# Loading four operands through GpSimd's queue into the tiles that they are split in

## The chip, the cores and the metric

The kernel runs on one core of one Trainium2 chip. The metric is the device time of one execution in microseconds (us); lower is better.

## What is computed

One layer of an encoder trunk on 1,024 tokens of width 1,024, with 16 learned meta tokens put in front. In outline:

```
a = rms_norm(h)
[q,k,v | q,f_fwd,f_bwd,i,g | gate_na, gate_hg] = a @ W_in
A  = W_na_out( neighbourhood attention(q, k, v) )
Bm = W_hg_out( bidirectional HGRN2 recurrence(q, f_fwd, f_bwd, i, g) )
h  = h + W_o( sigmoid(gate_na) * A + sigmoid(gate_hg) * Bm )
h  = h + W_down( relu(rms_norm(h) @ W_up)^2 )
out = rms_norm(h), meta tokens dropped
```

The change lies in the two gates, `sigmoid(a @ W_gate)` for 2,048 columns.

## The kernel before

Every float32 product is made as three products of float32r operands: an operand is split into a high part (a rounded copy, made by ScalarE) and a low part (the operand minus its high part, made by VectorE). The helper is `split(hi, lo, src)`, lines 95 to 97: line 96 is ScalarE's copy, line 97 VectorE's subtraction. Both parts must be there before TensorE can use the operand.

The stages follow one another: norm and transposition of `a` into the tiles `aT` (two halves of 512 tokens, each with a high and a low tile of 128 x 8 x 512), the recurrence (to about 350 us), attention in four pairs of heads (to about 597 us), the gates, the two output projections, the MLP. The gates use Winograd's seven products for 2 x 2 blocks. The activations' blocks are `b11` and `b21` (the first half of the tokens as it stands in `aT`), `b22` (the lower half of the second) and four sums of blocks, `t1` to `t4`, the second operands. The sums are made piece by piece during attention by `block_sums`: GpSimd adds high and low parts back together, subtracts, and stores each of the 4 x 4 pieces (128 x 512 float32, 256 KB) in DRAM as `tsp[v][k]`.

In the gates stage the first two products of each of eight column pairs need `b11` and `b21` alone; they are `first_gates`, each with its own weight block (`load_block`: SP loads `raw`, line 125 is ScalarE's copy `hi`, line 126 VectorE's subtraction `lo`). Eight blocks pass through two pairs of `hi` and `lo` buffers, so a block's parts are made just when the block before the last has been used up. Then `gate_pair` runs eight times with the other five products, in the order b22, t2, t1, t3, t4 (the last one delayed behind the next pair's first). Before these stands `second_operand(v)`, for t2, t1, t3 and t4 in this order: for each of its four pieces SP loads `tsp[v][k]` into a staging tile `gv`, of which there are five, and `split` makes the high and low pieces from it. `t2`'s parts go into the upper halves of the second `aT` tiles (the projections of attention and `block_sums` have to be done with them); `t1`, `t3` and `t4` have tiles of their own, called `at` in the trace, in the pool `gpr`. The five `gv` tiles are used again in `gate_pair` for its results `u1`, `u3`, `u2`.

The pool `gpr` takes the place of attention's pool `npr`; both end where the pool `gfp` begins. By the sizes in the code `npr` has 46,912 bytes a partition (`Vn` 9,216, then `OT` 4,096, five `pr` of 1,728, small tiles, `PT0` and `PT1` of 11,264 each, `low` 2,048) and `gpr` 53,248 (six `at` tiles of 8,192, two `p3` of 2,048), so `gpr` starts 6,336 bytes below `npr`. `t1`'s low tile then covers bytes 1,856 to 10,048 of `npr`, the end of `Vn` and the beginning of `OT`; `t3`'s high tile covers `OT` and `pr`, its low tile `pr` and `PT0`; `t4`'s tiles cover `PT0` and `PT1`. A tile is written for the first time when the tiles that lay there are done with; `OT` is done with when its store to DRAM (`osp`, line 673, on GpSimd's queue) has landed.

The order of the instructions on each engine is not that of the code up to the last product of the MLP: a planner orders them by its own estimate of durations, takes the earliest in the code among those that it takes to be ready, and lets later ones go ahead into gaps. On the chip each engine, and each engine's DMA queue, then works strictly in that order.

Of the kernel before, what the change touches and what calls it, by code (L numbers as in the profile page):

```python
# [9 lines left out]
F32 = mybir.dt.float32  # L10
F32R = mybir.dt.float32r
# [7 lines left out]
P = 128  # L19
# [3 lines left out]
TH = 512  # L23
# [25 lines left out]
def layer(ctx: ExitStack, tc: tile.TileContext, x, meta, w_in, w_na, w_hg, w_o, w_up, w_dn,  # L49
          g_mix, g_mlp, g_fin, gain, bias, lbl, lmask, wmask, out):  # L50
    nc = tc.nc
    pe, act, dve, pool, sp = nc.tensor, nc.scalar, nc.vector, nc.gpsimd, nc.sync
# [42 lines left out]
    def split(hi, lo, src):  # L95
        act.copy(hi, src)  # L96
        dve.tensor_tensor(lo, src, hi.bitcast(F32), op=ALU.subtract)  # L97
# [128 lines left out]
    tsp = {v: [dramp.tile([P, TH], F32, name=f"tsp_{v}_{k}") for k in range(4)] for v in ("t1", "t2", "t3", "t4")}  # L226
# [301 lines left out]
    with (tc.tile_pool(name="npr", bufs=1, side="right", reuse_waits="tile") as npr,  # L528
# [18 lines left out]
        for p in range(NPAIR):  # L547
            NB = npl.tile([P, 2, 1024], F32, tag="NB", name="NB")
            for i in range(2):
# [3 lines left out]
                for o, j0, m in ((0, 0, 3), (432, 1, 2), (720, 0, 2)):  # L553
                    a = NB[:, i, o:o + m * SW].rearrange("p (j c) -> p j c", c=SW)[:, :, :P]
# [140 lines left out]
    def up_bank(t):  # L695
# [4 lines left out]
    aV = {"b11": [t[:, :4, :TH] for t in aT[0]], "b21": [t[:, 4:, :TH] for t in aT[0]],  # L700
          "t2": [t[:, :4] for t in aT[1]], "b22": [t[:, 4:] for t in aT[1]]}
# [5 lines left out]
    def flat(t):  # L707
        return t.rearrange("p k c -> p (k c)")
# [25 lines left out]
    gpr = gps.enter_context(tc.tile_pool(name="gpr", bufs=1, side="right", reuse_waits="tile"))  # L734

    def g_tile(tag, n, dt=F32, bufs=1):
        return gp.tile([P, n], dt, tag=tag, name=tag, bufs=bufs)

    def second_operand(v):
        for k in range(4):  # L740
            t = g_tile("gv", TH, bufs=5)
            if v not in aV:
                aV[v] = [gpr.tile([P, 4, TH], F32R, name=f"a{v}{q}") for q in range(2)]
            sp.dma_start(t, tsp[v][k])
            split(aV[v][0][:, k], aV[v][1][:, k], t)

    w_turn = [0]

# [54 lines left out]
    for v in ("t2", "t1", "t3", "t4"):  # L803
        second_operand(v)
# [25 lines left out]
    for br, wsrc in enumerate((w_hg, w_na)):  # L830
        for jj in range(0, KC, 2):
            raw, hi, lo = (flat(wp.tile([P, KC, P], dt, tag=t, name=t))
                           for t, dt in (("raw", F32), ("hi", F32R), ("lo", F32R)))
# [5 lines left out]
            for j in (jj, jj + 1):  # L839
                sg = sgp.tile([P, T], F32, tag="sg", name="sg")  # L840
                sp.dma_start(sg, gsp[8 * br + j])
                for h in range(2):
                    pm = mm_tile()
                    t = slice(h * TH, (h + 1) * TH)
# [119 lines left out]
    def a_tile(pool_, tag, dt=F32, bufs=1, n=TH):  # L964
        return pool_.tile([P, n], dt, tag=tag, name=tag, bufs=bufs)
# [89 lines left out]
    for m in range(NP):  # L1055
# [3 lines left out]
        for v in ("s1", "s3"):  # L1059
            t = a_tile(upw, "sx", bufs=2, n=D).rearrange("p (k c) -> p k c", c=P)  # L1060
# [215 lines left out]
    with tc.manual_schedule(engines={sp.engine, dve.engine, act.engine, pool.engine}):  # L1276
# [5 lines left out]
        for n, (p_, m) in enumerate(steps):  # L1282
# [13 lines left out]
            elif m < NP // 2 - 2:  # L1296
                a, b = cur
# [72 lines left out]
```

## Time and profile before

| what | value |
|---|---|
| median of 3 runs | 1552.63 us (1550.44 to 1553.09) |
| profiled execution: its time | 1550.2 us |
| profiled execution: span from first to last instruction | 1548.4 us |
| TensorE (PE) busy | 1502.1 us, 97% of the span |
| VectorE (DVE) busy | 1008.4 us, 65% |
| ScalarE (ACT) busy | 654.7 us, 42% |
| GpSimd (POOL) busy | 401.8 us, 26% |
| mean granted clock of TensorE | 0.998 of 2.4 GHz |

The profiled execution took 1.8 us more than its span and 2.4 us less than the median. In the rows, a time is counted from the start of the span; "idle before" is how long the engine had nothing to do ahead of an instruction, and behind the arrow stands what ended it. SPq, POOLq and ACTq are the DMA queues of SyncE, GpSimd and ScalarE.

### The profile page before, as it was taken

How to read it: one execution, taken by the hardware profiler on the slowest of the kernel's cores; microseconds unless marked ns; L12 is line 12 of the kernel's file. 1: busy time of each engine (PE TensorE's matmuls, PEld its weight loads, DVE VectorE, ACT ScalarE, POOL GpSimd, SP SyncE). 2: the span in 40 equal slices, each digit the busy share in tenths (PEclk: the TensorE clock that was granted, in tenths of full speed). 3: DMA queues.
4: the chain of work that ended last, by engine and by line, in shares of the span. 5: the costliest groups of instructions: out<-in, count | busy, mean ns of one | idle time of the engine just before them, and what ended most of it. 6: DMA issues, size and time to landing. Idle time of an engine off the chain costs nothing.

```text
span 1548.4 us, 23448 instructions
## 1 busy us (share of the span) xinstructions
PE 1502.1 (97%) x9188; PEld 1253.5 (81%) x9188; DVE 1008.4 (65%) x1592; ACT 654.7 (42%) x1168; POOL 401.8 (26%) x359
## 2 busy tenths in 40 slices
PE   6999999999999998999999999999999999999998
PEld 5788888878888887888888887888888788887886
DVE  6666666664876877666475369666666444879566
ACT  6231313124665666334122245555555433434444
POOL 4413131315315310011000032444444200237033
PEclk9999999999999999999999999999999999999999
DMA  5101010113123128434951324444444576563224
GB/s 181 43 28 56 28 56 28 55 29 128 49 72 119 55 69 272 136 123 163 339 178 41 109 91 148 165 155 153 153 150 148 169 273 233 190 231 107 98 82 150
DMA packets 142335, 195.61 MB, mean 126 GB/s; under 512 B 8064, under 2 KB 90112, under 8 KB 142224
## 3 DMA queue, kind: packets, MB, share of 16 engines
q1 hardware_dynamic: 133856, 173.40, 33.8%
q10 hardware_dynamic: 6192, 13.37, 2.2%
q0 software_dynamic: 2176, 7.34, 1.3%
q8 instruction: 72, 1.18, 0.3%
q14 instruction: 39, 0.32, 0.1%
HBM read 139.55 MB, written 54.53 MB: 125 GB/s over the span
## 4 chain that ended last, share of the span: by engine, by line
PE 83%; DVE 9%; issue 3%; ACT 2%; DMA 2%; POOL 1%; DVEq 0%; POOLq 0%; SPq 0%; ACTq 0%
PE mm L135 11%; PE mm L136 10%; PE mm L137 10%; PE mm L1112 4%; PE pa L1112 4%; PE pb L691 4%; PE pb L692 4%; PE pb L693 4%; PE pc L1112 4%; PE pb L1112 4%; PE pc L693 2%; PE pc L692 2%; PE pc L691 2%; PE pa L692 2%; PE pa L691 2%
## 5 line engine op out<-in xcount | busy, mean ns | idle before, releaser
L135 PE MATMUL mm<-aT,hi 128*128 128x512 f32 (+2 forms) x640 | 230.2, 360 | 2.7 <-DVE QX L563 1.5
L137 PE MATMUL mm<-aT,lo 128*128 128x512 f32 (+2 forms) x640 | 227.8, 356 | 0.0
L136 PE MATMUL mm<-aT,hi 128*128 128x512 f32 (+2 forms) x640 | 226.6, 354 | 0.0
L97 DVE TENSOR_TENSOR dl<-ur,dh 128x1024 fp32r<-128x1024 f32 x55 | 76.6, 1393 | 93.7 <-ACT dh L96 93.5
L135 PEld LDWEIGHTS mm<-aT,hi 128*128 128x128 f32 x640 | 121.9, 191 | 17.2 <-issue 1.7
L137 PEld LDWEIGHTS mm<-aT,lo 128*128 128x128 f32 x640 | 121.8, 190 | 13.5 <-POOL lo L126 0.3
L136 PEld LDWEIGHTS mm<-aT,hi 128*128 128x128 f32 x640 | 121.9, 190 | 12.4
L96 ACT CAST dh<-ur 128x1024 fp32r<-128x1024 f32 x55 | 57.9, 1053 | 162.5 <-issue 78.1
L125 ACT CAST hi<-raw 128x1024 fp32r<-128x1024 f32 x36 | 37.8, 1051 | 106.7 <-PE mm L136 75.6
L974 ACT CAST wh<-sx 128x512 fp32r<-128x512 f32 x70 | 42.5, 618 | 94.7 <-DMA sx<-in_w_up 33.1
L975 DVE TENSOR_TENSOR wl<-sx,wh 128x512 fp32r<-128x512 f32 x70 | 51.2, 738 | 31.0 <-ACT wh L974 31.0
L975 DVE TENSOR_TENSOR wl<-raw,wh 128x512 fp32r<-128x512 f32 x46 | 50.2, 1090 | 23.7 <-ACT wh L974 22.9
L979 ACT ACTIVATE uv<-uv 128x512 f32<-128x512 f32 x48 | 30.4, 632 | 67.4 <-DVE uv L1090 50.0
L1095 POOL TENSOR_TENSOR us<-u,uv 128x512 f32<-128x512 f32 x15 | 24.0, 1603 | 133.4 <-ACT uv L980 133.4
L1202 POOL TENSOR_TENSOR w<-w,tt 128x512 f32<-128x512 f32 x16 | 23.3, 1458 | 134.0 <-DVE tt L1201 120.4
L399 POOL TENSOR_TENSOR Y<-X,TN 128x512 f32<-128x512 f32 x20 | 35.0, 1749 | 86.1 <-DVE X L396 86.1
L691 PE MATMUL pb<-nt,wh 128*128 128x512 f32 x128 | 50.4, 394 | 3.6 <-DVE uv L1083 2.6
L126 DVE TENSOR_TENSOR lo<-raw,hi 128x1024 fp32r<-128x1024 f32 x34 | 43.2, 1270 | 15.6 <-ACT hi L125 15.4
L92 POOL TENSOR_SCALAR rtm<-ssq 128x1 f32<-128x1 f32 (+1 forms) x17 | 6.4, 376 | 180.4 <-ACT junk L924 156.0
L618 DVE CUSTOM_DVE_ANT_0 pr<-nsc,NB 128x432 f32<-128x432 f32 (+1 forms) x64 | 35.2, 559 | 26.6 <-PE nsc L613 26.5
L1112 PE MATMUL mm<-dl,dh 128*128 128x512 f32 x126 | 49.9, 396 | 2.1 <-DVE dl L97 2.1
L135 PE MATMUL mm<-o,hi 128*128 128x512 f32 x128 | 50.0, 390 | 0.6 <-DVE mix L850 0.6
(380 smaller groups left out, 4409.3 us busy)
## 6 DMA issues: line engine op xcount, KB each, us to landing
raw<-in_w_in SPq DMA_DIRECT2D x56, 512.0 KB, 3.9
ur<-usp SPq DMA_DIRECT2D x55, 512.0 KB, 3.5
raw<-in_w_up SPq DMA_DIRECT2D x16, 1024.0 KB, 5.5
usp<-us SPq DMA_DIRECT2D x60, 256.0 KB, 2.0
sg<-gsp SPq DMA_DIRECT2D x16, 512.0 KB, 4.3
w<-in_w_dn SPq DMA_DIRECT2D x16, 512.0 KB, 4.5
usp<-uv SPq DMA_DIRECT2D x30, 256.0 KB, 2.2
gsp<-gv ACTq DMA_DIRECT2D x24, 256.0 KB, 2.4
```

Source lines behind the costliest of these rows:

```text
L96: act.copy(hi, src)
L97: dve.tensor_tensor(lo, src, hi.bitcast(F32), op=ALU.subtract)
L126: eng.tensor_tensor(lo[:, :kc], raw[:, :kc], hi[:, :kc].bitcast(F32), op=ALU.subtract)
L135: pe.matmul(ps, lh, rh, start=first, stop=False)
L136: pe.matmul(ps, lh, rl, start=False, stop=False)
L137: pe.matmul(ps, ll, rh, start=False, stop=last)
L691: pe.matmul(ps, lhs[0][:, c], rhs[0][:, k], start=first and k == 0, stop=False, skip_group_check=True)
L692: pe.matmul(ps, lhs[0][:, c], rhs[1][:, k], start=False, stop=False, skip_group_check=True)
L693: pe.matmul(ps, lhs[1][:, c], rhs[0][:, k], start=False, stop=k == 3, skip_group_check=True)
L974: act.copy(v(hi), src)
L975: dve.tensor_tensor(v(lo), src, v(hi).bitcast(F32), op=ALU.subtract)
L1112: pe.matmul(ps, a[n == 2][:, q, j * P:(j + 1) * P], b[n == 1][:, q], start=first and n == 0, stop=last and n == 2, skip_group_check=True)
```

## The change

`second_operand` has no staging tile any more. The tiles of `t1`, `t3` and `t4` are made at the start. Each piece is loaded by GpSimd's queue instead of SP's, straight into the place of its low part; `split` then copies the high part from there, and the subtraction overwrites the loaded piece with the low part. The five `gv` tiles stay for `gate_pair`.

```
     def second_operand(v):
+        if v not in aV:
+            aV[v] = [gpr.tile([P, 4, TH], F32R, name=f"a{v}{q}") for q in range(2)]
         for k in range(4):
-            t = g_tile("gv", TH, bufs=5)
-            if v not in aV:
-                aV[v] = [gpr.tile([P, 4, TH], F32R, name=f"a{v}{q}") for q in range(2)]
-            sp.dma_start(t, tsp[v][k])
-            split(aV[v][0][:, k], aV[v][1][:, k], t)
+            hi, lo = (t[:, k] for t in aV[v])
+            pool.dma_start(lo.bitcast(F32), tsp[v][k])
+            split(hi, lo, lo.bitcast(F32))
```

## Rows read from the trace of the kernel before

**Rows 1.** The page: busy time of the engines, and the chain that ended last by engine.

```profile
PE 1502.1 (97%) x9188; PEld 1253.5 (81%) x9188; DVE 1008.4 (65%) x1592; ACT 654.7 (42%) x1168; POOL 401.8 (26%) x359
...
PE 83%; DVE 9%; issue 3%; ACT 2%; DMA 2%; POOL 1%; DVEq 0%; POOLq 0%; SPq 0%; ACTq 0%
```

**Rows 2.** Busy time by stretches of the span: end of attention, its tail, `first_gates`, the first gate pair, the other pairs. Columns: stretch, its length, then busy us of PE, PEld, DVE, ACT and POOL with counts, granted clock, DMA share, GB/s.

```profile
555.00:575.00 20.00, 19.96 (x122) 16.86 (x122) 19.02 (x58) 15.30 (x39) 0.00 (x0) 1.00 0.12 34
575.00:590.00 15.00, 12.57 (x71) 10.01 (x70) 12.26 (x32) 12.91 (x24) 0.00 (x0) 1.00 0.65 218
590.00:613.00 23.00, 21.10 (x96) 16.93 (x94) 16.69 (x26) 15.23 (x27) 0.54 (x1) 1.00 0.84 270
613.00:640.00 27.00, 26.91 (x119) 22.30 (x120) 16.39 (x23) 10.78 (x17) 1.60 (x1) 1.00 0.51 151
640.00:740.00 100.00, 99.62 (x439) 81.99 (x438) 63.79 (x82) 42.06 (x56) 12.01 (x7) 1.00 0.46 148
```

**Rows 3.** What TensorE waited for from 555 to 640 us (total us, times, longest).

```profile
PE ppt L633 <- DVE PT L645: 2.4, 1, 2.4
PE mm L691 <- ACT hi L125: 1.5, 1, 1.5
PE mm L693 <- DVE lo L126: 0.5, 1, 0.5
```

**Rows 4.** The chain of waits in order of time, the load and what follows it on ScalarE (start, us, what).

```profile
602.40 6.04 DMA gv<-tsp_t
...
610.25 0.59 ACT go L712
```

**Rows 5.** ScalarE's instructions in order of time (start, us).

```profile
600.74 0.61 ACT L96 CAST at<-gv 128x512 fp32r<-128x512 f32 x1
601.25 0.62 ACT L96 CAST at<-gv 128x512 fp32r<-128x512 f32 x1
...
602.73 1.66 ACT L96 CAST at<-gv 128x512 fp32r<-128x512 f32 x3
604.96 0.59 ACT L724 COPY g<-mm 128x512 f32<-128x512 f32 x1 [0.57 <-PE mm L693]
608.46 1.88 ACT L96 CAST at<-gv 128x512 fp32r<-128x512 f32 x3 [2.91 <-DMA gv<-tsp_t]
...
610.74 1.04 ACT L125 CAST hi<-raw 128x1024 fp32r<-128x1024 f32 x1
```

**Rows 6.** VectorE's instructions in order of time, in attention's tail.

```profile
585.72 0.69 DVE L660 COPY low<-pov 64x512 f32<-64x512 f32 x1 [1.57 <-PE pov L658]
586.34 0.68 DVE L682 TENSOR_TENSOR sx<-raw 128x512 f32<-128x512 f32 x1
587.05 0.68 DVE L662 TENSOR_TENSOR OT<-pov,low 64x512 f32<-64x512 f32 x1
587.65 1.27 DVE L645 TENSOR_TENSOR PT<-ppt,PT 128x512 fp32r<-128x512 f32 x2
```

**Rows 7.** The instructions on the tiles `gv` (duration in ns min/median/max, first and last start in us).

```profile
L744 SPq DMA_DIRECT2D gv<-tsp_t x16: 319/354/1073, 581.5 to 610.5; - x16
L96 ACT CAST at<-gv x12: 610/622/631, 600.7 to 616.7; 128x512 fp32r<-128x512 f32 x12
L97 DVE TENSOR_TENSOR at<-gv,at x12: 684/689/694, 601.7 to 617.4; 128x512 fp32r<-128x512 f32 x12
...
L786 DVE TENSOR_TENSOR gv<-gv,pc x8: 678/680/689, 633.8 to 727.6; 128x512 f32<-128x512 f32 x8
```

**Rows 8.** What SP's queue waited for from 560 to 640 us (total us, times, longest).

```profile
SPq L744 <- DVE aT L97: 3.5, 4, 2.0
...
SPq L744 <- DVE at L97: 2.7, 4, 1.3
```

**Rows 9.** TensorE's first matmuls with t2 (`aT`, into `pb`), t1, and t4 (`at`) in the first gate pair.

```profile
626.37 0.39 PE L691 MATMUL pb<-aT,hi 128*128 128x512 f32 x1
...
629.09 0.39 PE L691 MATMUL pc<-at,hi 128*128 128x512 f32 x1
...
637.25 0.39 PE L691 MATMUL pb<-at,hi 128*128 128x512 f32 x1
```

**Rows 10.** GpSimd's instructions in order of time.

```profile
597.07 0.54 POOL L673 DMA_DIRECT2D osp<-OT  x1 [50.74 <-DVE OT L662]
636.50 1.60 POOL L790 TENSOR_TENSOR gv<-gv,p 128x512 f32<-128x512 f32 x1 [38.90 <-DVE gv L789]
```

**Rows 11.** DMA issues of the whole span (KB each, median us from issue to landing).

```profile
tsp_t<-rt POOLq DMA_DIRECT2D x16, 256.0 KB, 2.4
gv<-tsp_t SPq DMA_DIRECT2D x16, 256.0 KB, 5.1
```

**Rows 12.** The DMA engines from 594 to 613 us: what they moved, and two kinds of issue in it.

```profile
DMA packets 5223, 5.67 MB, mean 299 GB/s; under 512 B 273, under 2 KB 3355, under 8 KB 5222
...
raw<-in_w_in SPq DMA_DIRECT2D x2, 512.0 KB, 6.6
osp<-OT POOLq DMA_DIRECT2D x1, 512.0 KB, 4.4
```

**Rows 13.** The chain of waits in order of time: the last projection of attention that the chain holds, and the last products of attention's values.

```profile
552.36 0.23 PE mm L136
...
593.79 0.23 PE pov L658
```

## The prediction

> **What bounds the kernel now.** I read the page first: TensorE is busy for 97% of the span and holds 83% of the chain that ended last [rows 1]. A change that leaves TensorE's work alone can only win what TensorE idles, so the second view is the busy time by stretches around the gates [rows 2]. From 613 us on TensorE is full: 26.91 of 27 us, then 99.62 of 100. What can be won lies before, in the 38 us from 575 to 613, where it is busy for 12.57 + 21.10 = 33.67 us: 4.33 us of idle time. The third view, TensorE's own waits, names all of it: 2.4 us in attention's tail for VectorE's PT, and 1.5 + 0.5 = 2.0 us in `first_gates` for a weight block's high part, then for its low part [rows 3].
>
> The chain of waits tells where the 2.0 us come from: a load of a second operand's piece, issued at 602.40, lands 6.04 us later; the casts of three pieces follow it, then a gate's sigmoid at 610.25, and only then the weight block's `hi` [rows 4, 5]. ScalarE's own order shows the same from its side: done with `g` at 605.55, it stands still for 2.91 us on a piece that has not landed, and the weight block behind it starts at 610.74 [rows 5]. So the change touches exactly what made one of the two waits. The other, in the tail, is VectorE's: `low`, a Winograd sum of the weights let in between, `OT`, and PT last [rows 6].
>
> **Removed: the staging tiles and SP's sixteen loads.** Sixteen loads of 256 KB leave SP [rows 7], and with them SP's waits for a free `gv` tile, 3.5 + 2.7 us behind VectorE's subtractions [rows 8]. SP's later weight loads may go out earlier by up to 6.2 us, but TensorE waits for none of them (rows 3 hold no DMA, and from 613 us it is full [rows 2]): 0. The first `u1` of `gate_pair` no longer waits for a staging tile; the last subtraction out of one starts at 617.4 and `u1`'s chain with t2 starts at 626.37 [rows 7, 9]: 0.
>
> **Kept: the splits.** Sixteen copies of 0.62 us and sixteen subtractions of 0.69 us [rows 7] remain. That the subtraction now overwrites its own input has no row on these tiles; the nearest, `gv<-gv,pc`, works in place and takes 0.68 us [rows 7], so 0 from either side.
>
> **Moved: the loads, to GpSimd's queue.** An issue there keeps GpSimd for 0.54 us, so sixteen cost 8.6 us of an engine that does nothing from 546 us (597.07 - 50.74) to 636 us but store `OT` once [rows 10]. What is queued behind them is the first gate pair's subtraction at 636.50; if the last load is issued before that, it costs nothing. Bounds of one load's time: 2.4 us for the same 256 KB stored by GpSimd, 6.6 us for a weight load in the crowded stretch [rows 11, 12]; SP's loads of these very pieces have 5.1 us [rows 11]. I take 5, the same as now, wherever the DMA engines are crowded.
>
> The Trainium skill, page "DMA: Bandwidth & Descriptors", section "Issuing engines are not separate DMA queues", says that transfers started by different engines run on the same 16 DMA engines and interleave, and that another issuing engine saves only the sequencer's time. The trace agrees as far as it goes: in 594 to 613 us, with 299 GB/s over all queues, GpSimd's store took 4.4 us [rows 12]. By the rule alone nothing is won at all; that is the second rival below.
>
> What can differ is when a load starts. **t2**: its target is the second `aT` tile, free once attention's last projection is through, at about 553 us [rows 13], and GpSimd has nothing else to do until 597 [rows 10]. I expect its four loads there, where the DMA engines are busy for 0.12 of the time [rows 2]; so 4 x 256 KB (0.262 MB each), 1.05 MB, leave the crowded stretch. TensorE needs t2 at 626.37 [rows 9]. **t1, t3, t4**: no ring of five tiles holds them back, but the memory does. t4's low tile and t3's are free when attention's last products are done, about 594 [rows 13]; t1's low tile only when `OT`'s store has landed, 597.07 + 4.4 = 601.5 [rows 10, 12], and t3's high tile too. Now the casts of `at` begin at 600.74 [rows 5]. TensorE needs t1 at 629.09 and t4 at 637.25 [rows 9], some 20 us after all this: a late piece costs nothing by itself, only through the weight block that stands behind its cast on ScalarE.
>
> **The sum.** *ScalarE's wait.* Between 0 won (it comes again) and 2.0 us won (rows 3: 1.5 + 0.5). Since a quarter of the pieces has been split long before, and t3 and t4 can be under way from 594 instead of in turns of five tiles, I take all of it: -2.0. *t2's splits in attention.* ScalarE and VectorE take them between 555 and 590 us. VectorE is busy for 19.02 of 20 us there [rows 2], and four subtractions are 4 x 0.69 = 2.8 us. Bounds: 0, if all four fall into its idle time, the 1.57 us before `low` and the 1.0 us left in 555 to 575 [rows 2, 6]; +2.8, if each holds up attention, and through it TensorE, as the Winograd sum of 0.68 us did at 586.34 [rows 6]. Some 2.6 us of idle time hold three of the four; I take one in the way: +0.7. Everything else 0. The sum is 1550.2 - 2.0 + 0.7 = 1548.9 us for the profiled execution's kind; that execution lay 2.4 us under the median of the runs, so 1551.3 us against 1552.63.
>
> **The rivals.**
>
> *Both waits go.* If the changed order in attention's tail also lets PT come in time, as little as moving the 0.68 us sum and the slack of `OT` could [rows 6], all 4.33 us [rows 2] are won: 1552.6 - 4.3 = 1548.3 us. For it: both waits are accidents of one order. Against it: the change has no hold on the tail; VectorE gets more to do there, not less.
>
> *Nothing is won.* The loads take as long in any queue, and ScalarE again stands before a piece that the planner thought landed; then 1552.6 us. For it: a load of 6.04 us [rows 4] where the planner evidently reckoned with less, and the same DMA engines. Against it: 1.05 MB fewer in the crowd. The section of the Trainium skill named above speaks for this rival.
>
> *ScalarE's wait grows (slower).* Place: GpSimd's queue at `OT`'s store. If the planner lets the store go first, or t1's loads ahead of the others, all twelve loads of t1, t3, t4 start at 601.5 instead of 581 to 610. They are 3.15 MB; with the two weight loads of 1.05 MB, 4.2 MB at 299 GB/s [rows 12] take 14.0 us, to 615.5. Where all casts stand ahead of the weight block, it starts at 615.5 + 0.6 = 616.1 instead of 610.74 [rows 5]: +5.4 us, 1558.0. With eight casts ahead, as many as now start before it (1 + 1 + 3 + 3 [rows 5]), the last of the eight pieces lands (8 x 0.262 + 1.05) MB / 299 GB/s = 10.5 us after 601.5, and the block starts at 612.6: +1.9. It passes 0.2% (3.1 us) when the block starts after 613.8, with nine or ten casts ahead of it. For it: t1 comes first in the code and is the last to get its memory. Against it: the planner takes what is ready, so t3's and t4's loads may pass t1's.
>
> **How the numbers follow.** 0.2% of 1552.6 is 3.1 us, about what a measurement of this kernel can tell from no change. Chances: the forecast 0.42 (own range 1549.3 with the wait gone and no subtraction in the way, less the runs' spread of 1.3, to 1553.4 with all four); both waits gone 0.19; nothing won 0.14; ScalarE's wait grown 0.25. Faster by over 3.1 us: the first rival and a little of the forecast, 0.23. Slower by over 3.1 us: most of the last, 0.24. The rest, 0.53, lies within. The range runs from 1547.5 (both waits gone, less part of the spread) to 1557.0, most of the way to the last rival's 1558.0.
>
> **What would show it.** Right: GpSimd's queue issues four loads before 580 us; ScalarE's wait of 2.91 us on a load is gone, the weight block's `hi` starts near 608.5 and TensorE's wait of 1.5 us on it is missing; TensorE's wait in the tail is between 2.4 and 3.1 us. Wrong: the last weight blocks' `hi` start after 611 us behind casts of `at`, with a DMA named as what they waited for; or t2's loads stand behind `OT`'s store at 597; or the wait for PT grows by more than 1 us; or the planner, with other work ready at other times, lays out attention's last pair anew, so that a wait turns up that no row here has.

## The result, and the profile after

The changed kernel is slower: 1557.08 us median of 13 runs (1553.3 to 1559.47), against 1550.58 us (1548.66 to 1553.55) of the kernel before on the same chip. The ratio is 1.0028, interval [1.0018, 1.0037], that is +4.3 us (+2.8 to +5.7). (The medians are 6.5 us apart and the means 5.2; the text goes by the ratio and its interval.) A second sample (e7 below) gave 1.0026 [1.0015, 1.0038]. The forecast was 1551.3 us with a range up to 1557.0; the price lies at the end that belonged to the rival "ScalarE's wait grows".

The profiled execution took 1557.4 us, with a span of 1555.6 us. Its busy time by stretches, the same stretches as in [rows 2] and one more (columns as there):

```profile
555.00:575.00 20.00, 18.55 (x108) 15.01 (x107) 18.72 (x56) 16.09 (x38) 0.00 (x0) 1.00 0.09 28
575.00:590.00 15.00, 14.18 (x80) 11.30 (x78) 12.56 (x37) 13.33 (x26) 0.00 (x0) 1.00 0.41 123
590.00:613.00 23.00, 21.46 (x95) 17.90 (x96) 14.02 (x21) 11.47 (x19) 7.03 (x13) 0.93 0.63 217
613.00:640.00 27.00, 25.40 (x109) 19.79 (x108) 17.37 (x24) 13.62 (x21) 0.00 (x0) 1.00 0.53 176
640.00:740.00 100.00, 99.78 (x440) 82.09 (x439) 65.16 (x84) 41.34 (x55) 12.65 (x8) 1.00 0.44 144
```

Everything is 1.3 to 1.5 us later here from some 75 us of the span on, long before any edited line, so a stretch doesn't hold quite the same work as before. Three readings hold all the same: TensorE idles 1.45 us in 555 to 575, where it was full; it idles 1.6 us in 613 to 640, where it was full; and the granted clock is 0.93 in 590 to 613. What TensorE waited for, from 540 to 645 us:

```profile
PE ppt L633 <- DVE PT L645: 2.1, 1, 2.1
PE nsc L612 <- DVE mn L618: 1.4, 1, 1.4
PE mm L693 <- DVE lo L126: 1.1, 2, 0.5
PE mm L135 <- DVE KL L572: 0.6, 1, 0.6
PE mm L691 <- ACT hi L125: 0.5, 1, 0.5
```

Against [rows 3]: the wait for PT is still there (2.1 after 2.4), the two waits for weight blocks' parts come to 1.6 us after 2.0, and a wait of 1.4 us for VectorE's `mn`, attention's scores of the last pair, is new. (`KL`'s 0.6 us is in both, ahead of the stretch of [rows 3].) ScalarE's order shows where the new wait and the old ones come from:

```profile
552.86 1.23 ACT L96 CAST aT<-aT 128x512 fp32r<-128x512 f32 x2 [3.55 <-DMA aT<-tsp_t]
555.18 0.62 ACT L96 CAST aT<-aT 128x512 fp32r<-128x512 f32 x1 [1.09 <-DMA aT<-tsp_t]
555.70 1.04 ACT L125 CAST hi<-raw 128x1024 fp32r<-128x1024 f32 x1
...
608.16 0.62 ACT L96 CAST at<-at 128x512 fp32r<-128x512 f32 x1 [0.71 <-DMA raw<-in_w_in]
...
614.46 1.03 ACT L125 CAST hi<-raw 128x1024 fp32r<-128x1024 f32 x1
...
618.23 1.05 ACT L125 CAST hi<-raw 128x1024 fp32r<-128x1024 f32 x1 [1.72 <-DMA raw<-in_w_in]
```

t2's first piece is not there when ScalarE comes to it; it stands still for 3.55 and 1.09 us, with a weight block and the last pair's exponentials behind it. Later the wait of 2.91 us on a load of `gv` [rows 5] is gone, but the last weight block now waits 1.72 us for its own load. GpSimd's order:

```profile
549.58 2.62 POOL L744 DMA_DIRECT2D aT<-tsp_t  x4 [1.78 <-PE mm L137]
600.16 0.54 POOL L673 DMA_DIRECT2D osp<-OT  x1 [47.96 <-DVE OT L662]
603.61 4.31 POOL L744 DMA_DIRECT2D at<-tsp_t  x8 [2.91 <-DMA osp<-OT]
608.38 0.55 POOL L744 DMA_DIRECT2D at<-tsp_t  x1 [0.47 <-DMA at<-tsp_t]
```

All twelve loads of t1, t3 and t4 stand behind `OT`'s store and wait 2.91 us for it to land: the place that the slower rival named.

### The profile page after: what moved, and what is told of

The parts are those of the page before. It is cut to its first block, busy times and chain, and to the rows that moved or that the text cites. A ratio compares the mean times of both kernels' runs of the same rounds, so it can differ in the third digit from the quotient of the medians.

```text
span 1555.6 us, 23434 instructions
## 1 busy us (share of the span) xinstructions
PE 1505.6 (97%) x9188; PEld 1255.4 (81%) x9188; DVE 1012.3 (65%) x1592; ACT 655.3 (42%) x1168; POOL 408.6 (26%) x375
## 4 chain that ended last, share of the span: by engine, by line
PE 81%; DVE 10%; issue 3%; DMA 3%; ACT 2%; POOL 1%; DVEq 0%; POOLq 0%; SPq 0%; ACTq 0%
PE mm L135 10%; PE mm L136 10%; PE mm L137 10%; PE mm L1112 4%; PE pa L1112 4%; PE pb L691 4%; PE pb L692 4%; PE pb L693 4%; PE pc L1112 4%; PE pb L1112 4%; PE pc L691 2%; PE pc L692 2%; PE pc L693 2%; PE pa L691 2%; PE pa L692 2%
## 5 line engine op out<-in xcount | busy, mean ns | idle before, releaser
L97 DVE TENSOR_TENSOR dl<-ur,dh 128x1024 fp32r<-128x1024 f32 x55 | 76.6, 1392 | 93.4 <-ACT dh L96 93.3
L693 PE MATMUL pb<-nt,wl 128*128 128x512 f32 x128 | 50.5, 395 | 0.0
```

The costliest lines, as they stand in the source:

```text
L693: pe.matmul(ps, lhs[1][:, c], rhs[0][:, k], start=False, stop=k == 3, skip_group_check=True)
```

## The experiments

Each kernel was timed against the kernel before on the same chip. The first eight and e11 differ from the changed kernel in `second_operand` alone; the table gives the queue and the place:

```
-            pool.dma_start(lo.bitcast(F32), tsp[v][k])
-            split(hi, lo, lo.bitcast(F32))
+            src = lo.bitcast(F32) if IN_PLACE else g_tile("gv", TH, bufs=5)
+            QUEUE.dma_start(src, tsp[v][k])
+            split(hi, lo, src)
```

| run | t2 | t1, t3, t4 | ratio to before |
|---|---|---|---|
| changed, e7 | GpSimd, in place | GpSimd, in place | 1.0028 [1.0018, 1.0037], 1.0026 [1.0015, 1.0038] |
| e1 | SP, staged | GpSimd, in place | 0.9990 [0.9980, 1.0000] |
| e2 | GpSimd, in place | SP, staged | 1.0008 [0.9996, 1.0020] |
| e3, e8 | SP, in place | SP, in place | 0.9995 [0.9983, 1.0006], 0.9999 [0.9989, 1.0009] |
| e4 | GpSimd, staged | GpSimd, staged | 1.0032 [1.0021, 1.0042] |
| e5 | GpSimd, in place | SP, in place | 1.0001 [0.9989, 1.0012] |
| e6 | SP, in place | GpSimd, in place | 1.0006 [0.9994, 1.0017] |
| e11 | SP, staged | SP, in place | 0.9988 [0.9976, 0.9999] |

**Place or queue (e1 to e4).** Three theories: A, t2's early splits; B, the twelve loads behind `OT`'s store; C, GpSimd's queue as such. The edits are those of the table.

> t2 goes as in the kernel before (SP's queue, staging tiles, split after the copy); t1, t3 and t4 go as in the changed kernel (GpSimd's queue, straight into the low parts' tiles). Theory A, t2's early splits stand on ScalarE and VectorE ahead of attention's last pair: the delay of 1.8 us between 555 and 575 us is gone, TensorE's wait of 1.4 us on mn too, and the kernel stands at +0.5 to +2.5 us over before instead of +4.3. Theory B, the twelve loads behind OT's store are the cost: it stands at +3 to +5 us, as the changed kernel, and TensorE's waits on the weight blocks around 615 us keep their 1.6 us or more.

> Only t2 goes by GpSimd's queue into its low part's tile; t1, t3 and t4 go as in the kernel before. Theory A: +1.5 to +4 us over before, the delay between 555 and 575 us of 1.8 us is there. Theory B: 0 to +1 us.

> No staging tiles, as in the changed kernel, but all sixteen loads on SP's queue: the queue alone is undone. Theory A, what counts is that t2's target is free early and so its splits go early, whatever queue loads it: +3 to +5 us as the changed kernel, t2's loads on SP before 560 us. Theory C, the cost is GpSimd's queue (slower issue, its place behind OT's store): within 1.5 us of before. Theory B would keep the loads of t1 waiting for OT's store, now in front of SP's weight loads: slower than the changed kernel by 1 to 3 us.

> Staging tiles as in the kernel before, but all sixteen loads on GpSimd's queue: the queue alone is moved. Theory A: within 1.5 us of before, since staging tiles come free only near 580 us and t2's splits stay late. Theory C: +3 us or more. Theory B: the loads no longer wait for OT's memory; within 1.5 us, unless they stand behind OT's store on the queue.

e3 has t2 as early as the changed kernel, and the same wait for `mn` (1.5 us), and loses nothing: A alone is out. e4 keeps the staging tiles and moves only the queue, and loses as much as the change, so the queue has a part in it (by another wait, as the next lines show). But e1 has twelve of the sixteen loads in GpSimd's queue and loses nothing either, which neither B nor a plain C allows.

e4's profile says what a queue can do. TensorE waited 7.6 us for PT. VectorE's order holds a Winograd sum (`sx`, line 682) ahead of PT, as before [rows 6], and the sum's operand was late. VectorE's longest wait, and two pieces of the chain (start, us, what):

```profile
DVE sx L682 <- DMA raw<-in_w_in: 5.2, 1, 5.2
```

```profile
578.96 10.76 DMA raw<-in_w_in
589.75 0.70 DVE sx L682
```

A weight load issued by SP at 578.96 took 10.76 us, with five loads of pieces, one for each staging tile, issued by GpSimd from 577.64 on beside it.

**The four combinations (e5 to e8).**

> All sixteen pieces are loaded in place as in the changed kernel; t2's four by GpSimd's queue, the other twelve by SP's. With the three kernels beside it this makes the four combinations of two queues for two groups of loads, in place each time. Differences are against the kernel before. Theory D (each group that goes by GpSimd's queue costs on its own, and the prices add): +0.5 to +2 us, and this kernel and the one with t2 on SP's queue together cost what the changed kernel costs. Theory E (the price is paid only where all sixteen are in GpSimd's queue): within 1 us. Theory F (t2's four early loads by GpSimd are the price: ScalarE stood 3.55 us for them at 549.30 us in the changed kernel): +3 to +5 us.

> All in place; t2's four pieces by SP's queue, the other twelve by GpSimd's. Theory D: +1.5 to +4 us. Theory E: within 1 us. Theory F: within 1 us. Under D the loads of the twelve start behind OT's store, and ScalarE's casts of the pieces at begin after 606 us of the span.

> The changed kernel once more, for a second profile and beside the other combinations on one chip. All theories: +3 to +6 us. What the second profile is to tell: whether the waits of the first one recur, that is ScalarE's wait of about 3.5 us for t2's first piece ahead of attention's last pair (theory F needs it), TensorE's wait of 1 to 1.5 us for VectorE's mn, and a stretch at the granted clock of 0.5 at 585 to 595 us. If the stretch at the low clock is there again and the waits are as short as before, the price is the clock after an idle TensorE and not the waits themselves.

> All sixteen in place by SP's queue once more. All theories: within 1.5 us, as the first time. Under the reading that a short idle stretch in attention's tail decides whether the clock falls, this kernel has a wait for PT under 1.5 us and no stretch at the clock of 0.5 between 540 and 640 us; a kernel with t2 early and a PT wait over 2 us has one.

Neither half alone is told from no change, and both together cost 0.26%: E by the letter, though the halves' intervals leave D room for most of it. F is out: e5 has the wait for `mn` (1.4 us) and no loss. e7 shows the changed kernel's waits again (PT 2.1, `mn` 1.4, `lo` 0.9, `hi` 0.5 us). e8, all in place on SP's queue, waits from 540 to 645 us:

```profile
PE nsc L612 <- DVE mn L618: 1.2, 1, 1.2
PE ppt L633 <- DVE PT L645: 0.8, 1, 0.8
...
PE mm L693 <- DVE lo L126: 0.6, 2, 0.3
```

The wait for PT is 0.8 us instead of 2.1, and from 600 to 640 us TensorE waits for nothing; nor does it in e3. Ahead of that, behind PT, both have short waits for `lo` and for a gate's copy (1.1 us together here, 1.2 in e3). The first has a plain cause in VectorE's order. The changed kernel, then e8:

```profile
588.77 0.69 DVE L660 COPY low<-pov 64x512 f32<-64x512 f32 x1 [1.63 <-PE pov L658]
589.39 0.69 DVE L682 TENSOR_TENSOR sx<-raw 128x512 f32<-128x512 f32 x1
590.11 0.68 DVE L662 TENSOR_TENSOR OT<-pov,low 64x512 f32<-64x512 f32 x1
590.72 1.27 DVE L645 TENSOR_TENSOR PT<-ppt,PT 128x512 fp32r<-128x512 f32 x2
```

```profile
586.84 0.69 DVE L660 COPY low<-pov 64x512 f32<-64x512 f32 x1 [1.02 <-PE pov L658]
587.57 0.68 DVE L662 TENSOR_TENSOR OT<-pov,low 64x512 f32<-64x512 f32 x1
588.17 1.27 DVE L645 TENSOR_TENSOR PT<-ppt,PT 128x512 fp32r<-128x512 f32 x2
589.58 0.69 DVE L682 TENSOR_TENSOR sx<-raw 128x512 f32<-128x512 f32 x1
```

With t2's loads on SP the planner puts the sum behind PT. That is an order, not a property of a queue, and it came out this way in all four runs with t2 in place on SP (e3, e6, e8, e14: 0.8 us each).

The clock is the other difference. The changed kernel from 590 to 595 and from 595 to 600 us, then e8 from 590 to 595 us (the third figure from the end is the granted clock):

```profile
590.00:595.00 5.00, 3.46 (x13) 2.92 (x14) 4.97 (x10) 2.45 (x5) 0.00 (x0) 0.70 0.25 85
595.00:600.00 5.00, 5.00 (x26) 4.23 (x26) 3.75 (x5) 1.64 (x2) 0.00 (x0) 0.96 0.62 180
```

```profile
590.00:595.00 5.00, 4.18 (x22) 2.94 (x21) 5.00 (x9) 2.22 (x5) 0.00 (x0) 1.00 0.36 97
```

In the changed kernel TensorE had idled 2.1 us for PT, and then had the lower of its two levels for a while, 1.2 instead of 2.4 GHz: 0.30 x 5 + 0.04 x 5 = 1.7 us of work lost, which is 3.4 us at half speed.

**The store, t2's staging, and a second look at before (e9 to e12).** e10 lays out the tiles in another order, so that t1's and t3's loads need not wait for `OT`'s store; e12 does the same with t2 staged; e9 is the kernel before.

```
-        if v not in aV:
-            aV[v] = [gpr.tile([P, 4, TH], F32R, name=f"a{v}{q}") for q in range(2)]
+        for u in (u for u in ("t4", "t3", "t1") if u not in aV):
+            aV[u] = [gpr.tile([P, 4, TH], F32R, name=f"a{u}{q}") for q in range(2)]
```

> The kernel before once more, for a second profile. Its measured time is the same by construction (within 1 us). What is open: the first profile had TensorE waiting 0.6 us for VectorE's mix at 747 us, and most profiles with an early t2 1.7 to 2.1 us. If that difference belongs to the change, the wait is again under 1 us here; if it varies from execution to execution, it may be 1.5 us or more. The waits of ScalarE's casts (TensorE's 1.5 and 0.5 us at 610 to 613 us) are expected again, and no wait for VectorE's mn at 553 us.

> The changed kernel with the tiles of t4, t3 and t1 laid out in this order instead of t1, t3, t4, so that t1's and t3's loaded pieces lie over PT0 and PT1 and no longer over OT, whose store stands just ahead of them in GpSimd's queue; only t4's loads still need that store to have landed. Theory G (the twelve loads are late because of the landing of OT's store, and that is the main part of the loss): GpSimd's first eight loads start within 1 us after the store's issue instead of 3.4 us, TensorE's waits between 605 and 622 us (1.4 to 1.6 us in the changed kernel) fall under 0.5 us, and the time is +1 to +3 us against before instead of +4. Theory H (the loss is t2's early splits in attention's last pair and the idle stretch in the tail, which this leaves): unchanged, +3 to +5 us, with the waits for mn and PT as in the changed kernel.

> t2's four pieces through the staging tiles as before, the other twelve in place; all sixteen by SP's queue. This should keep what the change can win (the twelve loads no longer wait for a staging tile) without t2's early splits and without GpSimd's queue. By the waits seen so far: no wait for mn (1.2 to 1.5 us saved against the other in-place kernels), PT wait as before (2.4 us), the waits of 2.0 us at 610 to 613 us gone. Theory H: -1 to -3 us against before, the fastest of all. If the early splits of t2 cost nothing on balance, it is no faster than the kernel with all sixteen in place on SP's queue (-0.5 us).

> t2 through the staging tiles by SP's queue as before; the other twelve in place by GpSimd's queue, with the tiles turned as in the kernel above (t4, t3, t1). Against the same without the turn (-1.6 us measured): theory G: another -0.5 to -1.5 us, the casts of the pieces at starting 3 us sooner and TensorE's waits of 1.1 and 0.9 us at 608 to 613 us gone; theory H: no difference beyond 0.7 us.

e10 did what its edit says: the eight loads follow `OT`'s store at once.

```profile
598.62 0.54 POOL L673 DMA_DIRECT2D osp<-OT  x1 [46.84 <-DVE OT L662]
599.15 4.31 POOL L744 DMA_DIRECT2D at<-tsp_t  x8
```

And it is no faster than the changed kernel: 1.0031 [1.0018, 1.0044]. The loads came sooner, and TensorE's wait for `hi` grew from 0.5 to 2.8 us, since the last weight block's load landed later. ScalarE in e10, then in e12:

```profile
614.18 1.04 ACT L125 CAST hi<-raw 128x1024 fp32r<-128x1024 f32 x1 [2.88 <-DMA raw<-in_w_in]
```

```profile
610.67 1.04 ACT L125 CAST hi<-raw 128x1024 fp32r<-128x1024 f32 x1 [4.04 <-DMA raw<-in_w_in]
```

e12 measured 1.0007 [0.9995, 1.0019], against 0.9990 for e1, which lacks the turn: again not better with earlier loads. Theory G is out; the time that H gave for e10 held. The time from issue to landing of the last weight blocks' loads (SP, line 123, those issued from 595 to 612 us) shows what became of them. In this order e10, the changed kernel, e8, and before:

```profile
DMA to landing us min/median/max: 11.7/12.4/13.0
```

```profile
DMA to landing us min/median/max: 4.7/8.3/11.9
```

```profile
DMA to landing us min/median/max: 4.8/4.9/5.1
```

```profile
DMA to landing us min/median/max: 6.2/6.6/7.1
```

In all seven profiles with the twelve loads in place on GpSimd's queue (changed, e1, e6, e7, e10, e12, e13) a weight load of this stretch took 11.5 to 13.2 us; in the others none took more than 7.1. On SP's queue the twelve are issued in order with the weight blocks, and ten of them behind the last one (e8: the last weight load goes out at 603.57, ten loads of pieces from 603.99 on). On GpSimd's queue the weight blocks don't hold them back; they are under way beside the one that ScalarE needs next.

e11, with no load on GpSimd and no early t2, has no wait for `mn`, and 0.7 + 0.5 us for the weight blocks: 0.9988 [0.9976, 0.9999], about 2 us faster than before and just clear of no change.

e9, the second profile of before, corrects the baseline itself. What TensorE waited for from 540 to 645 us:

```profile
PE ppt L633 <- DVE PT L645: 2.4, 1, 2.4
PE mm L135 <- DVE KL L572: 0.6, 1, 0.6
PE mm L693 <- DVE lo L126: 0.5, 1, 0.5
```

The 1.5 us for `hi` of [rows 3] are not there: ScalarE stood 1.37 us for a piece instead of the 2.91 of [rows 5]. And its wait for VectorE's `mix` near 745 us, the first projection's product with a gate, was 2.5 us, where the first profile had 0.6: that wait is not the change's doing, as I had held possible.

**A turn of the staging tiles (e13, e14).** The wait for `mix` hangs on SP's first load of `sg`, which waits for the store of the last gate to land. Which staging tile that gate lies in depends on how often the five were used before; the sixteen uses of `second_operand` no longer count. Both runs add one use:

```
+    pool.memset(g_tile("gv", TH, bufs=5)[:, :1], 0.0)
     last = lambda: None
```

> The changed kernel with one more use of a staging tile (GpSimd writes one column of it, and nobody reads it), so that each later use takes the next of the five. Theory J (which of the five holds the last gate decides whether the first load of sg waits for that gate's store to land, so taking t2's and the other pieces' sixteen uses away changed that wait by accident): TensorE's wait for mix near 750 us falls from 1.7 to 2.1 us to under 0.9 us, SP's wait for the landing of gsp falls from 7.7 us to under 5 us, and the time comes down by 1 to 2.5 us to about +2 us against before. Theory K (that wait is set by something else that an early t2 shifts): wait and time as in the changed kernel, +3 to +5 us.

> All sixteen in place by SP's queue, with the same one more use of a staging tile. Theory J: the wait for mix under 0.9 us, and -1.5 to -3 us against before (without the turn: -0.6 us over two samples). Theory K: -0.6 us, within 1 us.

SP's wait for the landing (total us, times, longest) from 720 to 756 us, in the changed kernel and in e13:

```profile
SPq L841 <- DMA gsp<-gv: 7.7, 1, 7.7
```

```profile
SPq L842 <- DMA gsp<-gv: 3.4, 1, 3.4
```

TensorE's wait for `mix` in e13 fell to 0.4 us (1.8 in the changed kernel), and the time to 1.0001 [0.9987, 1.0016]: J for the changed kernel by the letter, and more of a fall (4.0 us between two ratios with intervals of 1.5 to 2.3 us on each side) than the wait. But a wait of 1.5 us for VectorE's `gv` in a gate pair stands in e13 where the changed kernel had 0.2 us, and 1.0 in e7:

```profile
PE pb L691 <- DVE gv L784: 1.5, 1, 1.5
PE mm L135 <- DVE mix L851: 0.4, 1, 0.4
```

e14 gave 0.9982 [0.9970, 0.9993], 2.8 us under before and the fastest of all, though its wait for `mix` was 1.4 us, over J's bound; so the time agrees with J there and the row does not. Nor does the turn decide the wait: by the code's count sixteen uses of five tiles leave the same turn as one, so e4, e13, e14 and the kernel before share it, and they waited 2.0, 0.4, 1.4 and, in before's two profiles, 0.6 and 2.5 us for `mix`. What made the times of e13 and e14 fall stays open: from the first scores of attention's last pair to the end of the span e13's profile takes 1001.5 us, as the changed kernel's do (1001.5 and 1002.3), and e14's 997.4, as e3's and e8's (997.1 and 997.0); but before's own two differ by 4.8 us over the same span.

e13 and e14 differ in the queue alone, and so do e7 and e8: 0.19%, 2.9 us, and 0.27%, 4.2 us, is what GpSimd's queue costs. The first of the two is only just clear of noise, by the two intervals.

## Why the prediction was wrong, point by point

**ScalarE's wait, -2.0: the step that failed.** What was taken away, the wait of 2.91 us on a piece, did go. Two things ate the gain. The 2.0 us were one execution's; e9 had 0.5 us there, so in the mean of the two 1.25 us were to be had. And a new wait took its place: the weight block's own load, 1.72 us on ScalarE, and 1.6 us (1.4 in e7) on TensorE in three places for the last two blocks. Their `hi` started at 614.46 and 618.23, after 611 us and the second with its own load as what it waited for, the sign of being wrong that the prediction had set. The step said that 1.05 MB leave the crowded stretch; it did not ask which loads had been kept behind the weight blocks by SP's order. With the same in-place tiles on SP's queue TensorE waits for nothing from 600 to 640 us in e3 and e8, and for 0.3 us in e5; but short waits of 1.1 to 1.2 us came ahead of that in e3 and e8, and the times of all three can't be told from before's. So the 2.0 us were not won on SP's queue either.

**t2's splits, +0.7: mis-sized, and in another place.** GpSimd issued the four loads at 549.58, as forecast. TensorE's wait for `mn` behind them was 1.4 us (1.4 again in e7, 0.5 to 1.5 in the other runs with t2 in place), within the bounds of 0 to 2.8. Not the length of VectorE's subtractions was in the way, as I had it: they stood ahead of the scores in VectorE's order and waited for ScalarE's casts, which stood 3.55 + 1.09 us before pieces that had not landed. VectorE's wait from 545 to 566 us (total us, times, longest):

```profile
DVE aT L97 <- ACT aT L96: 6.1, 2, 5.1
```

The planner put them there; I had asked only where TensorE needs t2. A wait that no row of before has was among the prediction's signs of being wrong.

**Everything else, 0.** The subtraction in place costs what the staged one did (0.69 us), and the first gate pair's subtraction on GpSimd is not held up: it starts at 641.40, 4.9 us after [rows 10] when TensorE itself is 4.8 us later. The wait for PT, 2.1 us, lies 0.3 us under the lower of the bounds given (2.4 to 3.1). That the planner might lay out the last pair anew was named; it did so when t2's loads were on SP, to the better. That nothing later hangs on how often the staging tiles were used, a 0 as well, is in doubt: one more use was worth 3.9 us between e7 and e13 and 2.6 us between e8 and e14, for a reason that the runs don't show.

**The rivals.** "Nothing is won" had the mechanism, but its price, zero, was too low: not only is the moved load no faster, the other queue's is slower, 11.5 to 13.2 us for a weight load. The section of the Trainium skill that it rested on ("DMA: Bandwidth & Descriptors", "Issuing engines are not separate DMA queues") says that transfers started by different engines interleave on the same 16 DMA engines. The slow weight loads agree. The rival with the chance 0.25 had the sign, and the twelve loads did stand behind `OT`'s store; but the cause it gave falls with e10, where the store no longer holds eight of them back and the kernel is as slow.

**The account.** In the mean of two profiles each, after against before shows +1.4 us for `mn`, -0.3 for PT and +0.2 for the weight blocks (1.6 and 1.4 against 2.0 and 0.5), and +0.9 for the stretch at 1.2 GHz in the tail, which both of after have and one of the two of before. That is 2.2 us of the 4.0 to 4.3 measured. The place is narrower than the waits tell. From the first scores of attention's last pair to TensorE's first product with t2, both profiles of before took 73.7 us and those of the changed kernel 77.0 and 76.6: 3.1 us of the loss lie here. Before (its second end is 626.37, [rows 9]), then the changed kernel:

```profile
552.65 0.29 PE L612 MATMUL nsc<-KS,QX 128*128 128x288 f32 x1
```

```profile
554.14 0.29 PE L612 MATMUL nsc<-KS,QX 128*128 128x288 f32 x1
...
631.14 0.39 PE L691 MATMUL pb<-aT,hi 128*128 128x512 f32 x1
```

From there to the end of the span before took 922.0 and 926.8 us, the changed kernel 924.5 and 925.7, which tells nothing. With all sixteen in place on SP's queue the stretch is back at 73.8, 73.2 and 73.5 us (e3, e8, e14); e5 has 73.5 and e6 75.3.

What is shown is that GpSimd's queue for all sixteen costs 2.9 to 4.2 us against SP's (e14 against e13, e8 against e7), and that this stretch is 3.5 and 3.4 us longer in these pairs. How that divides among `mn`, PT, the clock and the late weight load is not shown: e1 has the late weight load (11.9 us) and 2.0 us of waits for ScalarE behind it, and is not slower than before; nor can e6, e12 and e13, which have it too, be told from before, though e12 and e13 took 76.9 and 77.0 us for the stretch. And why one more use of a staging tile gave e13 its 3.9 us back stays open.

## What to carry to other kernels

An in-order queue is also a priority: loads that stand in it behind the urgent ones start behind them (4.8 to 5.1 us for the last weight loads of e8, up to 11.9 in the changed kernel). Before moving loads to an idle engine's queue, list which loads of the old queue they stood behind, and count their bytes beside those. And take a second profile before pricing a wait of one or two microseconds; a wait that only one execution shows is no gain to be had.

## What the runs showed that I had not expected

A weight load of 512 KB issued between 595 and 612 us took 3.9 to 7.1 us where t1, t3 and t4 came by its own queue. Where eight or nine of their loads ran from another at once, one or both of the two weight loads took 11.5 to 13.2 us. With the ring of five staging tiles holding them back (e4) the weight loads of that stretch took 5.6 to 6.1 us; the one beside five loads, 10.76.

An idle stretch of TensorE can cost more than its length, and not each time. Of twelve profiles with a wait for PT of 2.1 us or more, eight show 1.2 GHz for 3.4 us or twice that right behind it (e4, after 7.6 us, 6.8), and four do not; the four with 0.8 us show none. One and the same wait of 2.6 us near 960 us, which all sixteen profiles have, was followed by it in nine. So the same kernel's profiles differ by 1.7 us at such a place.
